# Moving every SBUF tile of a two-layer backbone step by 96 bytes: a pad removed on one side, four constant tiles merged into one on the other

## The chip, the cores and the metric

The kernel runs on one core of a Trainium2 chip. The metric is the device time of one execution in microseconds, the median over several runs. One further execution was profiled; its rows are the ones read below.

## What is computed

The reference runs two layers (DEPTH 2) over 1152 tokens, 1024 of a sample and 128 of a prompt, with a model width of 1024. In short:

```python
def mix_inputs(x, cond, p):
    h = rmsnorm(x, p["g_norm"]) * (1 + scale) + shift      # shift, scale, gate from silu(cond) @ w_mod
    return gate, jnp.split(h @ p["w_in"], ...)             # one wide projection, columns for all branches
...
# three branches: a bidirectional gated scan (rnn), latent attention (mla), windowed attention (swa)
u = (m0 * ((y_rnn * silu(g_rnn)) @ p["w_br_rnn"])
   + m1 * ((y_mla * silu(g_mla)) @ p["w_br_mla"])
   + m2 * ((y_swa * silu(g_swa)) @ p["w_br_swa"]))
x = x + gate * (u @ p["w_out"])
```

A final RMSNorm follows, and the context's keys, values and scan states are outputs too.

## The kernel before

Every large product is made in three matmuls per block: each operand is split into a high part, rounded to float32r, and a low part, the rest. `mm3` (L235 to L241) issues, for each block k of 128 rows, high times high, high times low and low times high, all added up in one PSUM bank. In `nc.tensor.matmul(ps, x, y)` the first operand x is the stationary one (the weight load of 128 columns ahead of each matmul), the second, y, is the moving one (its 384 columns stream through).

The work of a layer runs in this order. The input stage multiplies 48 blocks of `w_in` with the normed states (`in_unit`, L240; results named `in`), 5 blocks token by token (`tm`), and between them the gates of the scan (`g`). Then the rnn branch's projection (`merge`, results `mgrnn`), the latent attention (queries `q`, keys `k`, scores `sa`, `sb`, `sm`, transposes `pt`, products `o`), the windowed attention (`ss`, `spt`, `so`) with the projection of the latent branch between (`mg`), the projection of the windowed branch (`mgs`) and the output projection (`out_unit`, results `wo`). TensorE's instructions stand in the order in which the program writes them (`tc.manual_schedule`). In the attention and in the first part of the kernel ScalarE, VectorE and GpSimd stand in a written order too; elsewhere the planner orders them. Weights come by DMA into `wr` (3 buffers); ScalarE makes the high part `wh` (L210) and GpSimd or VectorE the low part `wl` (L216), with two buffers each, while TensorE works on the block before.

Tiles lie in SBUF as stacks of pools from two sides. Each tile's bytes per partition are rounded up to a multiple of 32, so a constant tile of 4 bytes takes 32. Pools with `side="right"` grow down from the top at 229376; all others grow up from 16512. The first thing on the right is a pool `edge` with one tile of 96 bytes that nothing uses (L199). On the left, pool `base` begins with `ident`, `ident_r` and `ones`, then the four tiles `eps_t`, `tiny_t`, `mhalf`, `e_t` (L249 to L256), then everything else. The large tiles are mostly multiples of 256 bytes, so their starting addresses, taken modulo 256 bytes, follow from what lies below or above them:

| tile (what for) | side | start mod 256, before | after |
|---|---|---|---|
| `wr`, `wh`, `wl` in pools `wp` and `fw` (weights of nearly all stages) | left | 32 | 192 |
| `hhi`, `hli`, `hhh`, `hlh` (normed states, high and low) | right | 128 | 224 |
| `uh`, `ul` (input of the output projection) | right | 128 | 224 |
| `cqh`, `cql`, `ckh`, `ckl`, `kh`, `kl`, `skh`, `skl`, `qt` (attention) | right | 128 | 224 |
| `qh`, `ql`, `v` (latent queries and values), `sph`, `spl` | left | 32 | 192 |
| `p`, `ph`, `pl` (latent probabilities) | left | 224 | 128 |
| `ymh`, `yml` (latent branch's output) | right | 96 | 192 |
| `yh`, `yl` (rnn branch, blocks 4 to 7) | left | 32 | 192 |
| `yxl`, `ygsil` (rnn branch, block 3) | left | 160, 64 | 64, 224 |
| `ysyA`, `ysyB`, `ysh`, `ysl` (windowed branch's output) | left | 32 | 192 |
| `wh_swa`, `wl_swa` in pool `fwp` | left | 128 | 32 |
| `twh`, `twl` (weights of `tm`, moving there) | left, right | 96, 128 | 0, 224 |
| `ident` (moving operand of the transposes) | left | 128 | 128 |

Steps inside these tiles (512 bytes from one stationary block to the next, 1536 bytes from one moving block to the next) are multiples of 256, so every matmul of a group has the start in the table.

Of the kernel before, what the change touches and what calls it, by code (L numbers as in the profile page):

```python
# [9 lines left out]
F32 = mybir.dt.float32  # L10
# [7 lines left out]
P = 128  # L18
# [10 lines left out]
EPS = 1e-6  # L29
# [155 lines left out]
def backbone(tc, a, depth):  # L185
    nc = tc.nc
    ctx = ExitStack()
    with ctx:
        _backbone(ctx, tc, nc, a, depth)


def _backbone(ctx, tc, nc, a, depth):
    def pool(name, bufs=1, side="left", space=None, stack=ctx):
        kw = {} if space is None else {"space": space}
        if space is None:
            kw["side"] = side
        return stack.enter_context(tc.tile_pool(name=name, bufs=bufs, reuse_waits="tile", **kw))

    pool("edge", side="right").tile([P, 24], F32, name="edge")  # L199
    base = pool("base")  # L200
    wp = pool("wp", bufs=2)
    dr = pool("dr", space=DRAM)
# [43 lines left out]
    nc.vector.tensor_copy(out=ident_r, in_=ident)  # L246
    ones = base.tile([P, P], F32, name="ones")
    nc.vector.memset(ones, 1.0)
    eps_t = base.tile([P, 1], F32, name="eps_t")  # L249
    nc.vector.memset(eps_t, EPS)  # L250
    tiny_t = base.tile([P, 1], F32, name="tiny_t")
    nc.vector.memset(tiny_t, float(2.0 ** -100))
    mhalf = base.tile([P, 1], F32, name="mhalf")
    nc.vector.memset(mhalf, -0.5)
    e_t = base.tile([P, 1], F32, name="e_t")
    nc.vector.memset(e_t, float(np.exp(1.0)))  # L256
    mask = base.tile([P, 2, P], F32R, name="mask")
    mask_f = wp.tile([P, 8, P], F32, tag="wr", name="mask_f", bufs=3)[:, 0:2]
    nc.sync.dma_start(out=mask_f, in_=a["mask"])
# [1665 lines left out]
```

## Time and profile before

| | |
|---|---|
| median of 3 runs | 3291.07 us (3285.95 to 3297.55) |
| the profiled execution | 3295.29 us, its span 3293.5 us |
| TensorE busy | 3194.5 us, 97% of the span, 19572 matmuls |
| VectorE, ScalarE, GpSimd busy | 55%, 47%, 44% |
| mean granted clock | 0.99 |

The span runs from the first to the last instruction of the profiled execution. [...]

### The profile page before, as it was taken

What the parts mean: (1) busy time and instruction counts of PE and PEld (TensorE: products, weight loads), DVE (VectorE), ACT (ScalarE), POOL (GpSimd) and SP (SyncE); (2) the same over time, 40 slices, a digit from 0 to 9 for tenths busy, and PEclk for the clock granted to TensorE, in tenths of its full rate; (3) what the DMA queues carried; (4) which work ended last, traced back from release to release, by engine and by line L of the source; (5) the groups of instructions that cost most, each with busy time, mean ns of one, the idle gap of its engine ahead of it and who ended that gap; (6) DMA issues with size and microseconds to landing.
All of it is one profiled execution on the core that took longest, in us unless ns stands there. A gap on an engine that the chain in (4) does not pass through costs nothing. (4 is left out here: it accounts for less than half of the span.)

```text
span 3293.5 us, 52185 instructions
## 1 busy us (share of the span) xinstructions
PE 3194.5 (97%) x19572; PEld 3065.7 (93%) x19572; DVE 1812.4 (55%) x3253; ACT 1549.0 (47%) x3061; POOL 1452.0 (44%) x1174
## 2 busy tenths in 40 slices
PE   7999999999999999999999999999999999999998
PEld 4999999999999999898989999999999999989998
DVE  5345544312336888987562444433332388898766
ACT  4344444343315777764243433334342277776532
POOL 3655554343313444555374444333331244445643
PEclk9999999999999999999999999999999999999999
DMA  5333333332442102457432222222234400045664
GB/s 212 102 98 102 94 96 112 96 106 95 134 147 68 29 26 51 122 173 239 164 112 92 82 78 73 81 81 78 80 101 149 133 20 25 25 110 156 187 199 134
DMA packets 246652, 351.06 MB, mean 107 GB/s; under 512 B 73216, under 2 KB 200832, under 8 KB 246144
## 3 DMA queue, kind: packets, MB, share of 16 engines
q1 hardware_dynamic: 246400, 347.73, 33.7%
q8 instruction: 154, 2.52, 0.3%
q14 instruction: 98, 0.80, 0.1%
HBM read 248.87 MB, written 98.78 MB: 106 GB/s over the span
## 5 line engine op out<-in xcount | busy, mean ns | idle before, releaser
L240 PE MATMUL in<-hhi,wh_in 128*128 128x384 f32 x1536 | 523.8, 341 | 6.3 <-ACT osg L733 4.6
L240 PE MATMUL in<-hli,wh_in 128*128 128x384 f32 x1536 | 522.7, 340 | 1.6 <-DVE hli L426 1.6
L240 PE MATMUL in<-hhi,wl_in 128*128 128x384 f32 x1536 | 522.1, 340 | 0.0
L216 POOL TENSOR_TENSOR wl_in<-wr_in,wh_in 128x1024 fp32r<-128x1024 f32 x94 | 235.2, 2504 | 332.1 <-ACT wh_in L210 256.0
L240 PEld LDWEIGHTS in<-hhi,wh_in 128*128 128x128 f32 x1536 | 290.0, 189 | 7.1 <-ACT osg L733 5.3
L240 PEld LDWEIGHTS in<-hli,wh_in 128*128 128x128 f32 x1536 | 289.7, 189 | 3.9 <-DVE hli L426 3.9
L240 PEld LDWEIGHTS in<-hhi,wl_in 128*128 128x128 f32 x1536 | 289.9, 189 | 0.0
L240 PE MATMUL in<-hlh,wh_in 128*128 128x384 f32 x768 | 261.6, 341 | 2.9 <-DVE hlh L426 2.9
L240 PE MATMUL in<-hhh,wl_in 128*128 128x384 f32 x768 | 261.3, 340 | 2.0 <-POOL wl_in L216 2.0
L240 PE MATMUL in<-hhh,wh_in 128*128 128x384 f32 x768 | 261.5, 341 | 0.2 <-ACT osg L733 0.2
L1168 POOL TENSOR_SCALAR p<-p,mx 128x1152 f32<-128x1152 f32 x128 | 157.9, 1234 | 200.8 <-DVE mx L1165 127.0
L1219 DVE TENSOR_TENSOR pl<-pt,ph 128x512 fp32r<-128x512 f32 (+1 forms) x320 | 201.5, 637 | 28.2 <-ACT ph L1215 25.5
L1215 ACT CAST ph<-pt 128x512 fp32r<-128x512 f32 (+1 forms) x320 | 170.6, 551 | 92.6 <-PE pt L1208 87.9
L609 DVE SCALAR_TENSOR_TENSOR r<-r,txl 128x1156 f32<-128x1156 f32 x16 | 31.3, 1959 | 322.0 <-ACT r L608 322.0
L733 ACT ACTIVATE osg<-in 128x384 f32<-128x384 f32 x144 | 69.0, 489 | 237.0 <-PE in L240 157.6
L1208 PE MATMUL pt<-ident,p 128*128 128x128 f32 x1152 | 170.8, 274 | 9.9 <-DVE kl L1078 4.3
L1208 PEld LDWEIGHTS pt<-ident,p 128*128 128x128 f32 x1152 | 133.5, 140 | 33.8 <-DVE pl L1219 11.0
L210 ACT CAST wh_in<-wr_in 128x1024 fp32r<-128x1024 f32 x96 | 99.9, 1044 | 129.7 <-PE in L240 93.0
L1233 PE MATMUL o<-ph,v 128*128 128x256 f32 x576 | 152.8, 292 | 0.0
L240 PEld LDWEIGHTS in<-hlh,wh_in 128*128 128x128 f32 x768 | 145.0, 189 | 4.3 <-DVE hlh L426 4.3
L240 PEld LDWEIGHTS in<-hhh,wl_in 128*128 128x128 f32 x768 | 144.9, 189 | 2.3 <-POOL wl_in L216 2.3
L1233 PE MATMUL o<-pl,v 128*128 128x256 f32 x576 | 145.5, 280 | 0.0
(450 smaller groups left out, 9591.9 us busy)
## 6 DMA issues: line engine op xcount, KB each, us to landing
wr_in<-in_w_fm SPq DMA_DIRECT2D x96, 512.0 KB, 3.6
sg<-osg SPq DMA_DIRECT2D x144, 192.0 KB, 1.9
wr_wm<-in_w_mod SPq DMA_DIRECT2D x32, 512.0 KB, 4.0
wr_wo<-in_w_out SPq DMA_DIRECT2D x32, 512.0 KB, 3.6
yr<-gsil SPq DMA_DIRECT2D x16, 576.0 KB, 2.8
msgrnn<-sg SPq DMA_DIRECT2D x48, 192.0 KB, 2.4
u<-msgrnn SPq DMA_DIRECT2D x48, 192.0 KB, 2.5
qr<-qs SPq DMA_DIRECT2D x36, 256.0 KB, 4.0
```

The lines of the kernel that those rows point to most:

```text
L210: nc.scalar.copy(out=hi, in_=src)
L216: eng.tensor_tensor(out=lo, in0=src, in1=f(hi), op=ALU.subtract)
L240: nc.tensor.matmul(ps, x, y, start=n == 0, stop=n == last)
L609: nc.vector.scalar_tensor_tensor(out=rr[d], in0=rr[d], scalar=1.0, in1=tt[d], op0=ALU.add, op1=ALU.mult)
L733: nc.scalar.activation(out=o, in_=ps, func=ACT.Sigmoid)
L1168: nc.gpsimd.tensor_scalar(out=pts[i], in0=pts[i], scalar1=mxs[i][:, 5:6], scalar2=1.0, op0=ALU.mult, op1=ALU.mult)
L1208: nc.tensor.transpose(ps[:, w:w + P], pts[q][:, k * P:(k + 1) * P], ident)
L1215: nc.scalar.copy(out=r["h", j][:, 0:width(j)], in_=r["t", j][:, 0:width(j)])
L1219: nc.vector.tensor_tensor(out=r["l", j][:, 0:width(j)], in0=r["t", j][:, 0:width(j)], in1=f(r["h", j][:, 0:width(j)]), op=ALU.subtract)
L1233: nc.tensor.matmul(O[:, 0:256], V[k][:, h % 4, :], x[:, 256 * i:256 * i + 256], start=k == 0 and e == 0, stop=k == 8 and e == 1)
```

## The change

The pad tile on the right goes, and the four 4-byte constants become columns of one tile of 8 floats (32 bytes). Everything on the right stands 96 bytes higher than before, and everything on the left from the constants on stands 96 bytes lower. Nothing else changes: the four memsets write the same four columns, now of one tile, and every reader of `tiny_t`, `mhalf` and `e_t` reads its column.

```diff
-    pool("edge", side="right").tile([P, 24], F32, name="edge")
     base = pool("base")
     wp = pool("wp", bufs=2)
...
     nc.vector.memset(ones, 1.0)
-    eps_t = base.tile([P, 1], F32, name="eps_t")
-    nc.vector.memset(eps_t, EPS)
-    tiny_t = base.tile([P, 1], F32, name="tiny_t")
-    nc.vector.memset(tiny_t, float(2.0 ** -100))
-    mhalf = base.tile([P, 1], F32, name="mhalf")
-    nc.vector.memset(mhalf, -0.5)
-    e_t = base.tile([P, 1], F32, name="e_t")
-    nc.vector.memset(e_t, float(np.exp(1.0)))
+    consts = base.tile([P, 8], F32, name="consts")
+    eps_t, tiny_t, mhalf, e_t = (consts[:, i:i + 1] for i in range(4))
+    for t, v in ((eps_t, EPS), (tiny_t, float(2.0 ** -100)), (mhalf, -0.5), (e_t, float(np.exp(1.0)))):
+        nc.vector.memset(t, v)
```

## Rows read from the trace of the kernel before

**Rows 1.** The page's first line and its list of engines: busy time, share, instructions.

```profile
span 3293.5 us, 52185 instructions
PE 3194.5 (97%) x19572; PEld 3065.7 (93%) x19572; DVE 1812.4 (55%) x3253; ACT 1549.0 (47%) x3061; POOL 1452.0 (44%) x1174
```

**Rows 2.** Windows by stage: length, then busy time and count per engine, granted clock, DMA.

```profile
30.00:900.00 870.00, 854.79 (x5003) 820.95 (x5002) 349.93 (x469) 363.24 (x556) 421.76 (x279) 0.99 0.33 106
1030.00:1350.00 320.00, 311.79 (x2218) 291.13 (x2217) 276.51 (x643) 234.13 (x588) 142.37 (x142) 1.00 0.15 36
1500.00:1650.00 150.00, 142.18 (x791) 138.71 (x790) 89.84 (x115) 46.16 (x74) 70.25 (x57) 0.99 0.62 203
1650.00:2500.00 850.00, 831.39 (x4924) 827.42 (x4923) 346.62 (x416) 335.25 (x521) 365.42 (x253) 0.99 0.27 89
```

**Rows 3.** What TensorE waited for: microseconds in total, times, longest; the longest three.

```profile
PE mod L309 <- DMA wm<-in_w_mod: 9.0, 2, 6.5
PE mgs L240 <- DVE wl_swa L216: 8.4, 6, 2.7
PE g L240 <- ACT xh L210: 5.6, 2, 4.1
```

**Rows 4.** Timeline of the start: VectorE's constants and their first reader.

```profile
0.93 0.06 DVE L250 MEMSET eps_t<- 128x1 f32 x1
...
0.96 0.06 DVE L256 MEMSET e_t<- 128x1 f32 x1
...
5.65 2.92 POOL L341 TENSOR_TENSOR ex<-e_t,na 128x16 f32<-128x16 f32 x1 [4.36 <-DVE na L339]
```

**Rows 5.** Groups by line and form, whole span: count, busy time and mean ns of one.

```profile
L240 PE MATMUL in<-hhi,wh_in 128*128 128x384 f32 x1536 | 523.8, 341 | 6.3 <-ACT osg L733 4.6 <-ACT hhi L423 1.6
...
L240 PE MATMUL in<-hlh,wh_in 128*128 128x384 f32 x768 | 261.6, 341 | 2.9 <-DVE hlh L426 2.9
...
L1208 PE MATMUL pt<-ident,p 128*128 128x128 f32 x1152 | 170.8, 274 | 9.9 <-DVE kl L1078 4.3 <-DVE pl L1219 3.3 <-DVE mx L1164 1.7
...
L240 PE MATMUL wo<-uh,wh_wo 128*128 128x384 f32 x384 | 130.9, 341 | 0.3
...
L1436 PE MATMUL spt<-ident,spt 128*128 128x128 f32 x496 | 73.6, 274 | 2.1 <-DVE spl L1444 1.1 <-DVE smx L1416 0.6 <-DVE qt L1360 0.4
...
L240 PE MATMUL mg<-yml,wh_mgmla 128*128 128x384 f32 x192 | 64.5, 336 | 0.0
...
L240 PE MATMUL mgrnn<-yl,wh_rnn 128*128 128x384 f32 x168 | 56.3, 335 | 0.0
...
L240 PE MATMUL q<-cqh,wl_uq 128*128 128x384 f32 x144 | 49.2, 342 | 1.2 <-POOL wl_uq L1104 1.2
...
L240 PE MATMUL mgs<-ysl,wh_swa 128*128 128x384 f32 x64 | 21.7, 339 | 1.1 <-DVE ysl L216 1.1
```

**Rows 6.** Windows of unbroken `in` matmuls (columns as in rows 2).

```profile
530.88:539.35 8.47, 8.47 (x49) 8.47 (x49) 8.37 (x6) 7.08 (x8) 4.86 (x2) 1.00 0.44 132
1800.01:1842.40 42.39, 42.39 (x241) 42.39 (x241) 32.03 (x26) 21.35 (x27) 20.42 (x10) 1.00 0.21 70
2497.00:2507.59 10.59, 10.59 (x61) 10.59 (x61) 0.00 (x0) 1.47 (x3) 0.00 (x0) 1.00 0.11 42
```

**Rows 7.** The same of `wo`, `mgrnn` (blocks 4 to 7), `mg`, `mgs`, and `mgs` between `wo`.

```profile
1552.29:1560.75 8.46, 8.46 (x49) 8.46 (x49) 7.41 (x8) 2.18 (x4) 5.02 (x4) 1.00 0.83 270
913.69:919.92 6.23, 6.23 (x37) 6.22 (x37) 1.50 (x5) 0.00 (x0) 0.00 (x0) 1.00 0.30 60
1498.07:1502.05 3.98, 3.98 (x24) 3.98 (x24) 2.73 (x3) 1.79 (x3) 3.67 (x6) 1.00 0.36 92
1518.75:1526.88 8.13, 8.13 (x48) 8.13 (x48) 6.29 (x11) 2.23 (x5) 5.03 (x5) 1.00 0.73 234
1592.54:1594.66 2.12, 2.12 (x13) 2.12 (x13) 1.21 (x2) 1.47 (x2) 0.91 (x1) 1.00 0.04 8
```

**Rows 8.** Groups of `mgrnn` in its stage, blocks 0 to 3.

```profile
L240 PE MATMUL mgrnn<-yxl,wh_rnn 128*128 128x384 f32 x42 | 14.6, 346 | 0.0
...
L240 PE MATMUL mgrnn<-ygsil,wh_rnn 128*128 128x384 f32 x42 | 14.2, 339 | 0.0
```

## The prediction

> **What bounds the kernel now.** I read the page's list of engines first: TensorE is busy for 3194.5 of 3293.5 us, the next engine for little more than half [rows 1]. The windows by stage say the same of each stage: in the two input stages TensorE works 854.79 of 870 us and 831.39 of 850 us, with VectorE, ScalarE and GpSimd under half; in the attention it is 311.79 of 320 us, though VectorE and ScalarE are at 276.51 and 234.13 us there [rows 2]. The waits of TensorE are small: the longest three kinds come to 23 us together [rows 3]. So the end is set by how closely the matmuls follow each other. The last thing I read is that spacing, in stretches of nothing but 128x384 matmuls [rows 6, 7]. The previous matmul still runs when a window begins, so a window holds one more than it starts, and the spacing is its length over the count less one:
>
> - `in`: 42.39 us / 240 = 176.6 ns; in two other places 8.47 / 48 = 176.5 and 10.59 / 60 = 176.5 [rows 6].
> - `wo`: 8.46 / 48 = 176.3 ns [rows 7].
> - `mgrnn`: 6.23 / 36 = 173.1 ns; `mg`: 3.98 / 23 = 173.0 ns; `mgs`: 8.13 / 47 = 173.0 ns [rows 7].
>
> [...] The groups over the whole span divide alike: 341 ns for `in` and `wo`, 342 for `q`, against 335 and 336 for `mgrnn` and `mg` [rows 5]. The shape, the type and the engine are the same in both classes. What the other engines do makes no difference: the three `in` windows have VectorE at 99%, 76% and 0% and the DMA at 0.44, 0.21 and 0.11, and agree within 0.1 ns [rows 6]. What differs is where the operands stand. The wide spacing goes with a moving operand at 128 mod 256 and weights at 32; the tight one with 32 and 32 (`mgrnn`), 96 and 32 (`mg`), 32 and 128 (`mgs`, from its third block on).
>
> **The change, part by part.**
>
> *The constants and the pad.* The pad has no instruction. The memsets are still four, 0.06 us each, all done at 1.02 us, and the first reader starts at 5.65 us, released by VectorE's `na`, not by them [rows 4]. One tile instead of four can at most make a reader wait for the last of the four: nothing.
>
> *The transposes.* Their moving operand `ident` stays, the stationary `p` goes from 224 to 128. `spt` stands at 128 already and takes 274 ns as `pt` does [rows 5]. I take nothing.
>
> *Moving on the right, weights on the left: `in`, `wo`, `q`.* Here both shift, the one by 96 up and the other by 96 down: moving at 224, weights at 192. The trace has no homogeneous stretch of that pair, so I bound it by what I can take from other pairs. I describe a pair by the weights' start less the moving start, mod 256: `in` has 160, and the tight stretches have 0 (`mgrnn`), 192 (`mg`) and 96 (`mgs`). The pair after has 224, between 192 and 0, both tight. One group has 224 now, `ygsil`, at 339 ns where `yxl` beside it, at 128, has 346 [rows 8]; blocks of other starts lie between, so I read only the order from it. Described by the moving start alone, mod 64, the tight stretches are at 32 and the wide at 0, and 224 is at 32 too. Both descriptions put the new pair with the tight ones. So the best end is the whole difference, 176.5 - 173.1 = 3.4 ns a matmul; the bad end is worked out under the rivals. I take the tight value, since the nearest pairs on either side show it.
>
> The counts: `in` has 3 x 1536 + 3 x 768 = 6912 matmuls, `wo` 3 x 384 = 1152, `q` 3 x 144 = 432, of which a row each stands in [rows 5]. 8496 x 3.4 ns = 28.9 us, of which `in` is 23.5. Not all of it arrives. Where TensorE stood still it will wait for the same DMA, cast or reduction; it is busy for 97% to 98% of these stages [rows 2], and after a wait the first matmuls are spaced by the wait. I take 93%: 27 us. The other engines have room: GpSimd, which makes the low parts, is at 421.76 of 870 us, and a block of weights, used by 72 matmuls, would be asked for after 12.5 us instead of 12.7.
>
> *Scores and keys.* They are such pairs too (moving `kh`, `kl` on the right, weights `qh`, `ql` on the left), 768 matmuls for `sa` and `sb` by the code. At 3.4 ns that is 2.6 us at best; VectorE is busy for 276.51 of 320 us there [rows 2], so between 0 and 2.6, and I take 0, because softmax must keep up first.
>
> *Left with left: `mgrnn`, `mg`'s weights, `mgs`.* In `mgrnn` and `mgs` both operands shift alike, so the difference stays; `mg` goes from 192 to 0, as `mgrnn` is now. By difference they cost nothing. By the moving start mod 64 they would go from 32 to 0 and become wide: 576 (`mgrnn`, blocks 4 to 7) + 576 (`mg`) + 576 (`mgs`) matmuls x 3.4 = 5.9 us. Bounds 0 and +5.9; I take 0, since `mgrnn` with 32 and 32 and `mg` with 96 and 32 agree to 0.1 ns although their moving starts differ by 64.
>
> *The sum.* -27 us on the profiled execution of 3295.29 us, which is 3268; that execution was 4.2 us above the median, so **3264 us** against 3291.07. What separates a change from none in this kernel is about 0.3%, some 10 us: its three runs spread by 11.6 us.
>
> **The rivals.**
>
> *No change (3291 us).* The spacing may belong to the place or the order of the matmuls and not to the start mod 256. For it: `mgs` between blocks of `wo` has 2.12 / 12 = 176.7 ns [rows 7], with the same starts as the stretch at 173.0 ns; so a pair that can be tight may be wide after wide ones, and starts alone don't decide. And all wide groups read their moving operand from tiles on the right. Against it: `mg` reads from the right too and is tight, and if `wo` becomes tight there is nothing wide left for `mgs` to follow. [...]
>
> *Part of it (about 3272 us).* The new pair is tight, but by the start mod 64: then the left pairs give back 5.9 us, and `o`, with moving `ph` going from 224 to 128, up to 2 more by the code's 1152 matmuls at half the length. -27 + 8 = -19.
>
> *Slower (3320 us).* The new pair is a worse one. The worst group of its shape is `yxl` at 346 ns, 5 above `in` [rows 5, 8]. If `in`, `wo` and `q` came to 180 ns, 3.4 more than now, it is +28.9 us, or 3320. It decides from a spacing of 176.6 + 10 / 8.5 = 177.8 ns on. For it: I have no stretch at 224 and 192, and the pair of `in` shows that starts which look harmless can cost. Against it: no homogeneous stretch here stands above 176.7.
>
> **How the numbers follow.** Tight with nothing given back 0.50, tight with part given back 0.20, no change 0.18, slower 0.12. Faster is 0.70, the same 0.18, slower 0.12. The likeliest gives 3264; its own range is 3256 (the scores' 2.6 us and the missing 7% besides, with the runs' scatter) to 3272. The range for 8 in 10 has to take in no change: 3255 to 3293. It leaves out the rival that ends slower and the tails.
>
> **What would show it.** After, the windows of unbroken `in` and `wo` should give 173 ns and their groups 335 to 337 ns; `mgrnn` and `mg` should keep 335 and 336; TensorE's busy time should fall by about the gain and its waits stay. The prediction is wrong if `in` stays at 176.5 ns (starts mod 256 don't matter, or history does), if it goes up, or if `in` is tight and the time stays, with waits of TensorE grown by some 20 us.

## The result, and the profile after

After the change the time is 3270.81 us (median of 4 runs, 3269.61 to 3271.97); the kernel before, in 4 runs, took 3294.14. The ratio is 0.9933, 95% interval 0.9912 to 0.9954: 23.3 us faster. The profiled execution of the kernel after took 3271.47 us. The page's first line and its list of engines:

```profile
span 3269.7 us, 52185 instructions
PE 3169.1 (97%) x19572; PEld 3039.1 (93%) x19572; DVE 1815.7 (56%) x3253; ACT 1547.4 (47%) x3061; POOL 1455.6 (45%) x1174
```

Beside [rows 1] the instructions are as many on every engine. TensorE's busy time fell by 25.4 us, the span by 23.8; VectorE, ScalarE and GpSimd changed by less than 4 us each. So TensorE does the same work in less time, and does not wait less. What TensorE waited for, the longest five (microseconds in total, times, longest):

```profile
PE mgs L239 <- DVE wl_swa L215: 8.9, 6, 2.7
PE mod L304 <- DMA wm<-in_w_mod: 8.3, 2, 7.0
PE g L239 <- ACT xh L209: 6.2, 2, 4.6
PE wo L239 <- POOL wl_wo L215: 6.1, 3, 3.6
PE in L239 <- ACT osg L728: 5.9, 3, 3.1
```

The three kinds of [rows 3] come to 23.4 us, as before to 23.0. Groups by line and form (count, busy time and mean ns of one); lines of the code now stand one to five lower:

```profile
L239 PE MATMUL in<-hhi,wh_in 128*128 128x384 f32 x1536 | 519.8, 338 | 6.7 <-ACT osg L728 5.1 <-ACT hhi L418 1.6
...
L239 PE MATMUL in<-hlh,wh_in 128*128 128x384 f32 x768 | 259.2, 337 | 2.3 <-DVE hlh L421 2.2
...
L1203 PE MATMUL pt<-ident,p 128*128 128x128 f32 x1152 | 171.0, 274 | 9.8 <-DVE kl L1073 4.2 <-DVE pl L1214 3.3 <-DVE mx L1159 1.7
...
L239 PE MATMUL wo<-uh,wh_wo 128*128 128x384 f32 x384 | 130.3, 339 | 0.5 <-ACT uh L209 0.5
...
L239 PE MATMUL mg<-yml,wh_mgmla 128*128 128x384 f32 x192 | 64.4, 335 | 0.0
...
L239 PE MATMUL mgrnn<-yl,wh_rnn 128*128 128x384 f32 x168 | 56.2, 335 | 0.0
...
L239 PE MATMUL q<-cqh,wl_uq 128*128 128x384 f32 x144 | 48.8, 339 | 1.3 <-POOL wl_uq L1099 1.3
```

Against [rows 5], `in`, `wo` and `q` are 2 to 4 ns shorter; `pt` is the same, `mg` and `mgrnn` within 1 ns. The windows show it more sharply. The durations in the rows overlap: those of `in` are 337 to 338 ns in the mean, while in the second window below the next matmul starts after 173.3 ns. So a window goes from the start of one matmul to the start of a later one, and I divide by the starts between. These are 48, 240, 239 and 60 of `in`, then 48 of `wo`, 36 of `mgrnn`, 23 of `mg` and 47 of `mgs`; the count in the row takes in one or two that were still running when the window began. (Columns as in [rows 2].)

```profile
529.60:537.91 8.31, 8.31 (x49) 8.31 (x49) 8.21 (x5) 7.14 (x8) 4.94 (x2) 1.00 0.45 127
1789.62:1831.22 41.60, 41.60 (x242) 41.60 (x241) 32.08 (x26) 21.34 (x27) 19.64 (x10) 1.00 0.21 71
859.83:902.06 42.23, 42.23 (x241) 42.23 (x241) 0.02 (x1) 8.63 (x15) 11.83 (x5) 1.00 0.48 166
2476.27:2486.67 10.40, 10.40 (x61) 10.40 (x61) 0.00 (x0) 1.47 (x3) 0.00 (x0) 1.00 0.12 43
1546.53:1554.85 8.32, 8.32 (x50) 8.32 (x50) 7.29 (x8) 2.18 (x4) 4.91 (x4) 1.00 0.74 249
908.35:914.60 6.25, 6.25 (x37) 6.22 (x37) 1.52 (x5) 0.00 (x0) 0.00 (x0) 1.00 0.31 62
1492.42:1496.41 3.99, 3.99 (x25) 3.99 (x24) 2.73 (x3) 1.79 (x3) 3.65 (x6) 1.00 0.33 86
1513.08:1521.23 8.15, 8.15 (x49) 8.15 (x48) 5.18 (x10) 2.33 (x5) 5.14 (x5) 1.00 0.75 234
```

`in` now runs at 41.60 / 240 = 173.3 ns where it had 176.6 [rows 6], at the same granted clock of 1.00, and `wo` at 8.32 / 48 = 173.3 where it had 176.3 [rows 7]. I call a spacing near 173.4 ns tight and one near 176.6 ns wide. `mgrnn` (173.6), `mg` (173.5) and `mgs` (173.4) are tight in their windows, as before. Over the whole span `mg` is not: most of it stands in groups of 12 between matmuls of the attention, 24 of these 40 groups now have 175 ns or more, where none had, and its mean rose from 173.4 to 174.8 ns. One row does not fit: the stretch of `in` at 859.83 still has 42.23 / 239 = 176.7 ns. Over the whole span `in` falls into such stretches: taken in groups of 24, 232 of 284 have 173.3 ns and 52 have 176.6, and none lies between. In the kernel before, the groups of `in` have 176.3 to 176.8.

Matmul by matmul (the 19572 stand in the same order in both traces), spacings that changed by no more than 20 ns add up to -23.8 us: `in` -18.5, `wo` -3.6, `q` -1.1, scores and all else -0.6 with +0.7 of `mg` among it. Larger changes, the waits, add up to -0.5 us.

### The profile page after: what moved, and what is told of

It reads as the page before. It is cut to its first block, busy times and chain, and to the rows that moved or that the text cites. A ratio compares the mean times of both kernels' runs of the same rounds, so it can differ in the third digit from the quotient of the medians.

```text
span 3269.7 us, 52185 instructions
## 1 busy us (share of the span) xinstructions
PE 3169.1 (97%) x19572; PEld 3039.1 (93%) x19572; DVE 1815.7 (56%) x3253; ACT 1547.4 (47%) x3061; POOL 1455.6 (45%) x1174
```

## The experiments

Theory D says that the spacing follows the weights' start less the moving operand's start, modulo 256. Its rivals are M (the moving start modulo 64 decides), W (the weights' start decides) and, later, history (what ran before decides). Two sizes set the starts: a pad on the right moves the moving operands of `in`, `wo` and `q` down, a larger constant tile moves the weights up. All edits are to the kernel after, with moving at 224 and weights at 192.

**Both halves of the change alone.** First, the pad removed but the weights left at 32 (moving 224, difference 64):

```diff
-    consts = base.tile([P, 8], F32, name="consts")
+    consts = base.tile([P, 32], F32, name="consts")
```

> Only the pad goes: normed states at 224, weights stay at 32 (weights less moving: 64). If the difference of the two starts decides (theory D), this kernel and the one with only the constants merged have the same difference and so the same spacing of the in matmuls, whatever it is. If the moving start alone decides, mod 64 (theory M), 224 is good: in at 173 to 174 ns, about 3271 us. If the weights' start alone decides, mod 64 (theory W), 32 is bad: in at 176.7 ns, about 3294 us. If history decides, nothing can be said of it.

Second, the constants merged but the pad kept (moving 128, weights 192, difference 64 again):

```diff
+    pool("edge", side="right").tile([P, 24], F32, name="edge")
     base = pool("base")
```

> Only the constants are merged: normed states stay at 128, weights at 192 (weights less moving: 64). D: the same spacing as with only the pad out. M: 128 is bad, in at 176.7 ns, about 3294 us. W: 192 is good, in at 173 to 174 ns, about 3271 us.

Measured: 3280.14 us, ratio 0.9969 (0.9956 to 0.9981), and 3285.77 us, 0.9978 (0.9966 to 0.9990), beside 3292.55 of before. Windows of 240 and of 48 starts of `in`, at the same places of the program, first with the pad removed, then with the constants merged:

```profile
1797.03:1838.95 41.92, 41.92 (x241) 41.92 (x241) 32.07 (x26) 21.35 (x27) 19.93 (x10) 1.00 0.21 71
533.14:541.62 8.48, 8.48 (x49) 8.48 (x49) 8.38 (x6) 7.13 (x8) 4.90 (x2) 1.00 0.39 127
```

```profile
1791.99:1833.91 41.92, 41.92 (x241) 41.92 (x241) 32.07 (x26) 21.35 (x27) 19.95 (x10) 1.00 0.22 71
532.27:540.75 8.48, 8.48 (x50) 8.48 (x49) 8.38 (x5) 7.12 (x8) 4.90 (x2) 1.00 0.45 131
```

The two kernels share neither start, only the difference, and these windows of `in` agree to the hundredth: 174.7 and 176.7 ns. Each half alone gives a part, and the parts are not independent: what counts is where the operands stand to each other.

Two things do not agree. The first block of `wo`, 48 starts, has 173.5 ns with the pad removed and 176.5 with the constants merged:

```profile
1551.88:1560.21 8.33, 8.33 (x50) 8.33 (x50) 7.33 (x8) 2.17 (x4) 4.95 (x4) 1.00 0.80 271
```

```profile
1546.71:1555.18 8.47, 8.47 (x49) 8.47 (x49) 7.57 (x8) 2.31 (x5) 4.72 (x4) 1.00 0.92 307
```

Over the span `wo` comes to 174.9 and 175.1 ns: in the first eight blocks of the first layer tight and wide ones take turns, and the two kernels begin with opposite ones. So at this difference both spacings occur, and something else than the difference picks one. And the times lie 5.6 us apart, with ranges that do not touch (3278.70 to 3281.22 and 3282.35 to 3291.73).

**The difference at 192.** Moving at 0, weights at 192:

```diff
+    pool("edge", side="right").tile([P, 56], F32, name="edge")
     base = pool("base")
```

> Constants merged and a pad of 224 bytes on the right: normed states at 0, weights at 192 (weights less moving: 192, that of the tight mg stretch before). D: in at 173 to 174 ns, about 3271 us. M: 0 is bad, 176.7 ns, about 3294 us. W: 192 is good, 173 to 174 ns.

**The difference of before, at other starts.** Moving stays at 224, weights at 128, so the difference is 160:

```diff
-    consts = base.tile([P, 8], F32, name="consts")
+    consts = base.tile([P, 56], F32, name="consts")
```

> No pad on the right, 192 bytes more on the left: normed states at 224, weights at 128 (weights less moving: 160, the difference of the kernel before). D: in at 176.7 ns as before, about 3294 us. M and W: 224 and 128 are both good, 173 to 174 ns, about 3271 us.

Measured: 3267.71 us, ratio 0.9931 (0.9916 to 0.9946), with the difference at 192; 3292.16 us, 0.9997 (0.9988 to 1.0007), with it at 160. The window of 240 starts and, in each, the one of `mg` with 23, first of the kernel with 192, then of the one with 160:

```profile
1787.44:1829.05 41.61, 41.61 (x242) 41.61 (x241) 32.07 (x26) 21.35 (x27) 19.63 (x10) 1.00 0.22 71
1488.56:1492.63 4.07, 4.07 (x25) 4.07 (x24) 2.78 (x3) 1.79 (x3) 3.65 (x6) 1.00 0.37 104
```

```profile
1796.54:1838.94 42.40, 42.40 (x242) 42.40 (x241) 32.03 (x26) 21.35 (x27) 20.43 (x10) 1.00 0.21 71
1498.28:1502.27 3.99, 3.99 (x24) 3.99 (x24) 2.73 (x3) 1.79 (x3) 3.65 (x6) 1.00 0.33 91
```

With 192 `in` has 41.61 / 240 = 173.4 ns, and all its 282 groups of 24 are tight. With 160 it has 42.40 / 240 = 176.7 ns, the 176.6 of before, though the moving start is the one of after: M falls, and the whole gain is gone with a larger constant tile alone.

**Four more differences.** The same pad with 8, 16, 32 and 40 floats: moving at 192, 160, 96 and 64, weights at 192 throughout.

```diff
+    pool("edge", side="right").tile([P, 8], F32, name="edge")
     base = pool("base")
```

> Constants merged, right pad of 32 bytes: normed states at 192, weights at 192 (difference 0). If the difference decides, as the four runs so far say, this is the pair of the mgrnn stretch of before: in at 173.1 to 173.3 ns throughout, about 3268 us. If instead only the two differences 192 and 224 are good for in (its operands come from other tiles than mgrnn's), it stays at 175 or above, 3280 us or more.

> Constants merged, right pad of 64 bytes: normed states at 160, weights at 192 (difference 32). Not seen in a pure stretch. Between the tight 0 and the mixed 64: some of the in blocks tight and some wide, 174 to 175.5 ns, about 3275 to 3283 us. If only 192 to 0 are good and all else is like 160: 176.7 ns and 3292 us.

> Constants merged, right pad of 128 bytes: normed states at 96, weights at 192 (difference 96, that of mgs in the kernel before, which was tight in one stretch and wide in another). If the difference decides and 96 allows both: in partly wide, 174 to 176 ns, about 3275 to 3288 us. By the weights' start or the moving start mod 64 it would be tight throughout, about 3268 us.

> Constants merged, right pad of 160 bytes: normed states at 64, weights at 192 (difference 128, next to the bad 160). If the difference decides: wide or nearly, 176 to 177 ns, 3286 to 3294 us. If the bad difference is 160 alone: mixed, 174 to 175.5 ns, about 3280 us.

The results, with `in` over the whole span (mean of the spacings below 190 ns):

| moving, weights | difference | `in`, ns | time, us | ratio to before (95%) |
|---|---|---|---|---|
| 192, 192 | 0 | 173.5 | 3272.20 | 0.9936 (0.9922 to 0.9951) |
| 160, 192 | 32 | 173.5 | 3279.81 | 0.9960 (0.9946 to 0.9975) |
| 224, 32 and 128, 192 | 64 | 175.5 and 175.3 | above | above |
| 96, 192 | 96 | 173.4 | 3276.97 | 0.9952 (0.9937 to 0.9967) |
| 64, 192 | 128 | 175.8 | 3289.55 | 0.9997 (0.9985 to 1.0008) |
| 224, 128 (before: 128, 32) | 160 | 176.7 (before: 176.7) | 3292.16 | 0.9997 (0.9988 to 1.0007) |
| 0, 192 | 192 | 173.3 | 3267.71 | 0.9931 (0.9916 to 0.9946) |
| 224, 192 (after) | 224 | 173.9 | 3270.81 | 0.9933 (0.9912 to 0.9954) |

The window of 240 starts with the difference at 0, 32 and 96, then at 128, where the second row is `mg`:

```profile
1789.16:1830.78 41.62, 41.62 (x242) 41.62 (x242) 32.01 (x26) 21.36 (x27) 19.62 (x10) 1.00 0.21 71
```

```profile
1790.05:1831.65 41.60, 41.60 (x241) 41.60 (x241) 32.08 (x26) 21.36 (x27) 19.63 (x10) 1.00 0.21 72
```

```profile
1790.10:1831.70 41.60, 41.60 (x241) 41.60 (x241) 32.02 (x26) 21.35 (x27) 19.62 (x10) 1.00 0.22 72
```

```profile
1801.86:1843.99 42.13, 42.13 (x242) 42.13 (x242) 32.09 (x26) 21.35 (x27) 20.17 (x10) 1.00 0.21 70
1500.07:1504.12 4.05, 4.05 (x24) 4.05 (x24) 2.77 (x3) 1.79 (x3) 3.65 (x6) 1.00 0.37 91
```

Both expectations of a mixed `in`, at 32 and at 96, missed: it is tight at both (2 of 284 groups are wide at 96). No edit moves the difference by as much as 256 bytes, so that it counts modulo 256 is not tested.

`wo` goes with `in`: 173.3 to 173.8 ns at 0, 32, 96, 192 and 224, 174.9 and 175.1 at 64, 176.0 at 128, 176.6 at 160. `q`, with 432 matmuls, does so only in part: it has 175.2 ns at 0 and at 32, where `in` has 173.5. So the difference isn't all that counts for it, and I tried nothing on `q` alone.

W falls too: with the weights at 192 throughout, the windows of `in` have 173.4 ns at difference 0 and 175.5 at 128. M falls a second time: 192 is 0 modulo 64 and is tight.

`mg` is a second witness, in its windows. Its moving operand stands 32 bytes lower than that of `in`, so its difference is 32 more. The row of `mg` in the kernel whose `in` has 128 (so 160 for `mg`) gives 4.05 / 23 = 176.1 ns, and in the kernel whose `in` has 160 (so 192) 3.99 / 23 = 173.5: in the one kernel both are wide, in the other `mg` is tight where `in` is wide. With `in` at 192 `mg` has 224, and its row above gives 4.07 / 23 = 177 ns (a hundredth of a us is 0.4 ns in these short windows). Over the whole span `mg` follows only in part: 173.4 and 173.5 ns where its difference is 192 (before, and with `in` at 160), 176.5 at 160, 175.9 at 128, but 174.6 to 174.8 at 0, 32 and 64, where `in` has 173.5 at the first two.

The times follow less closely than the spacing. At differences 32 and 96 `in` is tight, but the ratios are worth 13 and 16 us, where difference 0 gave 21; their profiled executions took 3270.22 and 3271.96 us, the lowest of the runs of each (up to 3280.44 and 3280.22). At 128 the profiled execution took 3300.79 us, the longest of ten: there small changes of spacing add up to -5.7 us and the waits to +11.0, of which 6.9 lie in the scores of the windowed attention. The mean granted clock goes with the time: at 32 the shortest execution had 0.992 and the other four, 7 to 10 us longer, 0.988 to 0.990; at 128 the longest had 0.989 and the shortest 0.991; the two kernels with 64 had 0.990 to 0.992 and, the longer one, 0.987 to 0.990. A share of 0.003 of 3280 us is some 10 us (an estimate from these numbers), about the size of these spreads. What makes the clock of one execution lower stays open, since one of each kernel is profiled.

**What makes some stretches of after wide.** In the kernel after, the 36 groups of `in` behind a gate chunk of 388 columns were all tight, while 23 of 72 behind chunks of 384 were wide. The next kernel makes the third chunk 384 columns too; it leaves out the last four columns of the gates.

```diff
-                    c0, c1 = c * CH, (c + 1) * CH if c < 2 else RW
+                    c0, c1 = c * CH, (c + 1) * CH
+                    if c == 2:
+                        nc.gpsimd.memset(dst[:, c1:RW], 0.5)
```

> The kernel after, with the third chunk of each gate of 384 columns instead of 388 (it leaves out the last four columns of the gates, which are set to 0.5). With the starts of after (weights less moving 224) most stretches of `in` ran at 173.3 ns and some 52 of 284 groups of 24 at 176.6. Every one of the 36 groups behind a gate's chunk of 388 columns was tight; behind chunks of 384 columns 23 of 72 were wide. If the matmul just ahead decides which of the two patterns a stretch falls into, some 10 or more of the 36 groups become wide, the mean of `in` rises from 173.9 to about 174.1 ns and the time stays within 2 us of after. If it is something else (the stage, the DMA at that moment), the 36 stay tight.

With it, on the same chip, ran the kernel with the difference at 192 and the kernel after once more:

> The kernel after with a pad of 224 bytes on the right (moving 0, weights 192, difference 192), beside the kernel after on the same chip. The difference decides: no stretch of `in` is wide, `in` at 173.3 ns against 173.9, which on 6912 matmuls is 4 us, less about 1 us that `mg` may give back: 2 to 4 us below after. If the two patterns of after are chance of one execution: both alike, within 1 us.

> The kernel after as it is. If its wide stretches follow from the order of its matmuls, they stand in the same places as in its first profile (the last blocks of the first input stage, the first blocks of the chunk ahead, the end of the second) and `in` is at 173.9 ns again; if they are chance, they stand elsewhere. Time 3270 to 3272 us.

Measured, beside 3294.35 us of before: gates of 384 columns 3274.83 us, ratio 0.9947 (0.9932 to 0.9962); difference 192 again 3270.91 us, 0.9933 (0.9920 to 0.9945); after again 3273.13 us, 0.9938 (0.9926 to 0.9950). Two stretches of `in`, of 215 and 239 starts, at the same places of the program, first with the narrower gates, then in the kernel after again:

```profile
181.04:219.02 37.98, 37.98 (x216) 37.89 (x216) 33.51 (x28) 16.73 (x22) 17.42 (x13) 1.00 0.21 68
862.57:904.79 42.22, 42.22 (x241) 42.22 (x241) 0.01 (x1) 8.63 (x15) 11.81 (x5) 1.00 0.49 165
```

```profile
180.26:217.53 37.27, 37.27 (x217) 37.18 (x216) 33.58 (x28) 16.68 (x22) 16.64 (x9) 1.00 0.21 69
858.70:900.13 41.43, 41.43 (x240) 41.43 (x240) 0.03 (x1) 8.63 (x15) 11.85 (x5) 1.00 0.51 169
```

The 36 groups behind the narrowed chunk stayed tight, so the width of the matmul just ahead does not decide. Yet history counts: the stretch at 181, which begins behind such a group and four small matmuls (`modT`), went from 37.27 / 215 = 173.3 to 37.98 / 215 = 176.7 ns with nothing changed but four columns of gates and the small GpSimd instruction that fills them. Six of the seven groups behind `modT` that can be read became wide, and none was in either execution of the kernel after; 86 of 282 groups were wide, and `in` rose to 174.3. The second stretch was wide in the first profile of after (the row at 859.83) and is tight in the second, 41.43 / 239 = 173.3. So chance has a part too: 31 of 282 groups were wide this time, against 52 of 284, and `in` has 173.7 ns. But the 23 groups behind gates are the same 23 in both executions, and all 31 are among the 52. Which stretch comes out wide is set partly by the order of the matmuls, partly by the execution; what rule lies behind it stays open.

`mg` at this difference has both spacings as well. In the repeat of the kernel with `in` at 192 its window, which had 4.07 us above, is this:

```profile
1488.27:1492.26 3.99, 3.99 (x25) 3.99 (x25) 2.73 (x3) 1.79 (x3) 3.66 (x6) 1.00 0.35 98
```

So a difference of 224 has two spacings, near 173.4 and 176.7, in two groups of matmuls with tiles and stages of their own. No group of `in` was wide with 192 in either run, but the times, 3270.91 (3268.64 to 3272.99) and 3273.13 (3269.79 to 3275.84), overlap: that 192 beats after is not shown.

## Why the prediction was right, and where its sizes were off

- *What bounds the kernel* held: the span fell by what the spacing of the matmuls gave, 23.8 us, and no other engine took the bound.
- *Difference, with 224 between two tight neighbours* held as a description for `in` and `wo`: their spacing over the span goes with the difference in all the kernels, and neither M nor W fits it. For `mg` it held in long windows, not over the span. The inference from neighbours was lucky, however. 64 stands between 32 and 96, both tight, and is mixed; 160 stands beside 192 and is wide. `ygsil` [rows 8] was weak evidence as well: it fell from 339 to 334 ns, and `yxl` from 346 to 342, though their differences stayed at 224 and 128.
- *`in` gains 3.4 ns* is the step that failed in size: it gained 2.7, 18.9 us by the mean against 23.5. The 52 wide groups account for 52 x 24 x 3.3 ns = 4.1 us, and the tight ones at 173.3 instead of 173.1 ns for another 1.1 (the sum is 0.6 more than what is missing, since `in` before was at 176.7 and not 176.5). The tight value was read too low: two windows of [rows 7] end some 0.02 us before the next start. Ended at it, `mgrnn` has 6.25 / 36 = 173.6 ns and `mgs` 8.15 / 47 = 173.4, where the prediction has 173.1 and 173.0, and the best end is some 3.2 ns instead of 3.4:

```profile
913.69:919.94 6.25, 6.25 (x38) 6.22 (x38) 1.52 (x5) 0.00 (x0) 0.00 (x0) 1.00 0.30 60
1518.75:1526.90 8.15, 8.15 (x48) 8.15 (x48) 6.31 (x11) 2.23 (x5) 5.05 (x5) 1.00 0.73 233
```

  That a group can stand at either spacing was there to see beforehand: `mgs` had both with one pair of starts [rows 7]. I took that for a neighbourhood of wide matmuls. The last section shows that the neighbourhood does decide there, but not by being wide.
- *`wo` and `q`*: 3.6 and 1.1 us, forecast 3.9 and 1.5.
- *93% arrives* was a wrong reason for a deduction that happened to be needed. The waits did not grow (-0.5 us); the shortfall lies in the spacing. All that the spacing gave arrived: GpSimd, busy for 1455.6 of 3269.7 us, kept TensorE waiting for low parts of the weights for 6.1 us in `wo`, 2.1 in `in` and 1.3 in `q`, where it was 3.0, 2.0 and 1.2 before.
- *Scores 0, left pairs 0, constants, transposes*: scores of 384 columns gave 0.65 us and all scores 1.5, `mgrnn` 0.0, `mg` +0.7, `pt` +0.1. All within the bounds.
- *The sum*: 3268 on the profiled execution, measured 3271.47. Against the median, 6.8 us lie between 3264 and 3270.81: 3.1 of them in the kernel before, whose median rose from 3291.07 to 3294.14 with the fourth run, and 3.7 are the gain of 23.3 instead of 27.
- *Rivals.* No change: with the order of the matmuls kept and the difference at 160 the whole gain is gone, so the order alone does not set the spacing. The kernels with differences 192 and 160 have `in` at 173.4 and 176.7 ns in their windows. That the spacing depends on the two starts together is what the runs show; by what means, no run here shows. Part of it, by the start modulo 64, had nearly the right time (3272) for a wrong reason: the left pairs gave back 0.7 us, not 5.9. Slower: no difference tried gave `in` more than 176.7.

## What to carry to other kernels

Where TensorE sets the end, measure the spacing of matmuls in unbroken stretches by shape, and compare groups of one shape: a difference of 3 ns on 8496 matmuls was the whole gain here, and it costs one pad to get. Look at the weights' start less the moving start, and try all eight multiples of 32 below 256 rather than infer one from its neighbours; a pad that is right for one pair can be wrong for another in the same kernel: with `in` at 192 `mg` has 224 and is wide in part. Where a spacing is seen in two values with the same starts, count what share of the matmuls has each before pricing the change.

## What the hardware showed that was not expected

- Starts that are all multiples of 32 bytes are not alike: a 128x384 float32r matmul of `in` takes 173.3 to 173.5 ns at differences 0, 32, 96 and 192, 175.3 to 175.8 at 64 and 128, and 176.7 at 160; the windows shown for it have a granted clock of 1.00.
- At 224 the same matmuls run at 173.3 or 176.6 ns for stretches of up to 239 matmuls, without change inside the stretch, and which of the two depends on what ran before and, in part, on the execution.
- The starts of the matmuls around a group count too. `mgs` between blocks of `wo` has one pair of starts in all kernels with the weights at 192, difference 96; only the moving operand of `wo` stands elsewhere. Over its 16 stretches it has 176.3 to 176.4 ns with `wo` at 192, 174.3 or 174.4 with `wo` at 224, 173.8 to 174.2 with it at 0, 32, 96 or 128, and 173.8 and 176.5 by turns at 64. `wo` itself is tight at 192 and wide at 128, so wide neighbours are not what makes it wide. The fourth stretch, 12 starts, with `wo` at 192, 224 and 128 (a hundredth of a us is 0.8 ns here):

```profile
1582.17:1584.29 2.12, 2.12 (x14) 2.12 (x14) 1.21 (x2) 1.48 (x2) 0.91 (x1) 1.00 0.00 0
```

```profile
1586.07:1588.16 2.09, 2.09 (x14) 2.09 (x13) 1.18 (x2) 1.48 (x2) 0.88 (x1) 1.00 0.00 0
```

```profile
1596.18:1598.27 2.09, 2.09 (x14) 2.09 (x13) 1.18 (x2) 1.47 (x2) 0.88 (x1) 1.00 0.04 8
```
